# A residual decoder block on one core: the modulation rows of the down projection on another queue, and one weight sum on VectorE

## The chip, the cores and the metric

One Trainium2 chip, one core of it. The core has TensorE (PE, with its weight loads listed as PEld), VectorE (DVE), ScalarE (ACT), GpSimd (POOL) and SyncE (SP). SP, POOL and ACT can each issue transfers between memory and the core's buffers; the bytes are moved by the core's 16 data engines. The time is device time in microseconds; the kernel runs the whole block in one launch, float32 in and out.

## The reference

One decoder layer over 512 tokens of width 1024. The part that matters here is the end of the second sub-layer:

```python
h2 = rms_norm(x, norm2_g[l]) * (1 + scale2) + shift2
u = causal_dwconv(h2 @ w_up[l], conv_w[l], conv_b[l])
u_g, u_v = jnp.split(u, 2, axis=-1)
x = x + gate2 * ((jax.nn.silu(u_g) * u_v) @ w_down[l])
```

`gate2` is the sixth of six rows of width 1024 that come from `mod = c_act @ ada_w[l] + ada_b[l]`. `w_down` has 2816 rows and 1024 columns. Everything before (the first norm, the combined projection, attention, pooling, the merged output projection) and the up projection are not touched by the change.

## The kernel before, in words

The product with `w_down`, which is called the down projection here, is computed by a scheme with seven products of half-size blocks in place of eight. The weight matrix is cut into blocks b11, b12, b22, b21, the activation into a11, a12, a21, a22, and sums of blocks are formed on both sides. The seven products run one after the other as seven phases; `phases` lists them with the PSUM accumulators (X, Y or Z, two banks each) that they add into: a11·b11, s1·t1, s2·t2, a12·b21, s3·t3, s4·b22, a22·t4. The sums of weight blocks are t1 = b11 + b12, t2 = t1 + b22, t4 = t2 + b21 and t3 = b12 + b22. (The signs are taken care of on the activation side.)

A phase walks over six units (`NU`) of the contraction. Units 0 to 4 are 1024 columns wide in the buffer (two halves of 512), unit 5 is 512. Each number is kept as a high and a low part, so a weight unit is first split: ScalarE copies it to the high part `hi`, VectorE subtracts to get the low part `lo`, and TensorE does three matmuls where one would do. With two halves and two output tiles, a unit is 12 matmuls of 128x512. Buffers for `hi` and for `lo` are four each, so the split of a unit waits until TensorE is done with the unit four before it.

The work on TensorE, VectorE and ScalarE runs in the order in which the program is written. What the weights need is written ahead of their use: `d_ahead` splits two units ahead of TensorE, and `d_load` stands two units ahead of the split. The order of SP's and POOL's queues is set by a scheduler that follows the waits and the same order. Each queue issues in order, and an entry that waits holds up those behind it.

How the weight sums are made before the change: b11 is loaded into eleven buffers `ta` of 128x512, which stay for the whole down projection. When b11 has been split, POOL issues, for each `ta`, a transfer that adds b12 to it while it lands (`accum_op=ALU.add`, line 1367); when t1 has been split, one that adds b22; when t2 has been split, one that adds b21. So there are 33 such accumulating transfers of 256 KB. t3 is made in a buffer `raw_t`: SP loads b12 into it, then POOL adds b22 by an accumulating transfer of 512 KB (line 1349). b21 and b22 are plain loads by SP into `raw_b`. `raw_t`, `raw_b` and the columns of `ada_w` for the modulation all come from one pool of five buffers (`load_unit`, line 82); a load waits until the buffer's last reader is done.

The row gate2 is made like this: `ada_col(5, k)` loads an eighth of its weights and VectorE sums it into a column of `acol` (line 202); the last three of the eight stand in the second phase. At the end of the second phase `row_of(5, "g2")` has POOL write the eight columns to a row `g_d` in memory (line 837) and then load that row, repeated over all partitions, into two buffers `g` (line 842). VectorE multiplies with them in `finish`, for the first time at the start of the fifth phase.

Of the kernel before, what the change touches and what calls it, by code (L numbers as in the profile page):

```python
# [15 lines left out]
P = 128  # L16
# [39 lines left out]
def block_kernel(tc, x, cvec, ada, wtok, wch, pool_w, wbr, wout, wup, wdn, pack, table, out):  # L56
# [4 lines left out]
    with ctx:  # L61
# [771 lines left out]

        def row_of(g, name):

            gd = dpool.tile([1, D], F32, name=f"{name}_d")
            nc.gpsimd.dma_start(gd.rearrange("o (k p) -> p (o k)", p=P), acol[:, 8 * g : 8 * g + 8])
            rows = []
            for f in range(2):
                r = slot(f"{name}_{f}")  # L840
                src = gd[:, f * 512 : f * 512 + 512]
                nc.gpsimd.dma_start(r, bass.AP(tensor=src.tensor, offset=src.offset, ap=[[0, P], [1, 512]]))
                rows.append(r)
            return rows
# [33 lines left out]
        for j in range(8):  # L878
# [19 lines left out]
            if j == 6:  # L898
                g1 = row_of(2, "g1")

# [432 lines left out]
        ta, draw, dready, done = {}, {}, {}, [0, 0]  # L1333
        NEXT = {"b11": "b12", "t1": "b22", "t2": "b21"}

        def d_load(m):
# [4 lines left out]
            if nm == "b11":  # L1341
                ta[i] = [slot(f"ta_{i}_{u}") for u in range(w // 512)]
                for u, t in enumerate(ta[i]):
                    nc.sync.dma_start(t, src("b11", u * 512, u * 512 + 512))
            elif nm[0] == "b":
                draw[m] = load_unit(src(nm), f"{nm}_{i}")
            elif nm == "t3":
                draw[m] = load_unit(src("b12"), f"t3_{i}")
                nc.gpsimd.dma_start(draw[m], src("b22"), accum_op=ALU.add)

        def d_split(m):
# [7 lines left out]
            else:  # L1359
                parts = [(t, slice(u * 512, u * 512 + 512)) for u, t in enumerate(ta[i])]  # L1360
            for t, cs in parts:
                nc.scalar.activation(hi[:, cs], t, AF.Copy)  # L1362
            for t, cs in parts:
# [119 lines left out]
        for n, (an, bn, acc) in enumerate(phases):  # L1483
            last = n == len(phases) - 1
            held_ = []
            for i in range(NU):
# [18 lines left out]
                elif n == 1:  # L1505
                    if i in (1, 3, 5):
                        ada_col(5, 5 + i // 2)
# [8 lines left out]
                elif n == 3:  # L1516
                    split_a("s4", i)
                    split_a("a22", i)
            if last:
                for p, c0, c1 in ((1, 0, 256), (0, 0, 256), (1, 256, 512), (0, 256, 512)):  # L1520
# [6 lines left out]
            elif n == 1:  # L1527
                keep("s5", "Y")
                g2 = row_of(5, "g2")
            elif n == 2:  # L1530
# [80 lines left out]
```

## Time and profile before

| what | value |
|---|---|
| median of 3 runs | 674.3 us (673.5 to 674.65) |
| the profiled execution's own time | 671.35 us |
| its span | 669.5 us |
| PE, share of the span | 97% |
| DVE | 85% |
| ACT | 58% |
| POOL | 19% |

In the page, a group row reads: line, engine, operation, output<-inputs, count, then busy time and mean of one in ns, then the idle time of the engine just before and what ended it. In the timeline a row begins with the start in microseconds and the duration. In the windows view each engine's busy time in a stretch is given, and behind it the granted TensorE clock (1.00 is full), the busy share of the data engines and the rate in GB/s. In a queue row stand packets, MB, and the share of the 16 engines' time; a share can be a little over 100% since packets overlap. A matmul's listed duration is longer than the step from one start to the next, since matmuls are pipelined.

### The profile page before, as it was taken

The page shows a single profiled execution, that of the slowest core. Times are in us where ns is not written, and L with a number is a line of the kernel's source. Part 1 is how long each engine was busy: PE and PEld are TensorE (multiplying, and loading weights), DVE is VectorE, ACT ScalarE, POOL GpSimd, SP SyncE. Part 2 cuts the span into 40 slices and gives each one's busy share as a digit, 9 for nine tenths or more (in the row PEclk, how much of TensorE's full clock was granted, in tenths as well). Part 3 has the DMA queues.
Part 4 walks back from the last instruction along what each step waited for, and adds up shares of the span by engine and source line. Part 5 has one row for each costly group of instructions (what it writes and reads, how often), then busy time and mean ns, then how long its engine had stood idle before and what let it go on. Part 6 is the DMA issues. An engine that isn't in the chain of part 4 may idle for free.

```text
span 669.5 us, 9758 instructions
## 1 busy us (share of the span) xinstructions
PE 650.9 (97%) x3469; PEld 559.9 (84%) x3469; DVE 568.2 (85%) x990; ACT 390.2 (58%) x701; POOL 130.5 (19%) x164
## 2 busy tenths in 40 slices
PE   8999999999999999999999999999999999993997
PEld 6788788888888888888988989889898888882886
DVE  7997887988878868999799799998998989981785
ACT  8564436766655556566675657566565648571441
POOL 3004063432100146423000000000000017532100
PEclk9999999999999999999999999999999999996899
DMA  8986259999732876476522133332332679999921
GB/s 348 324 314 242 73 195 285 284 306 310 206 135 96 260 180 219 159 266 237 172 82 94 67 123 106 104 107 80 109 127 95 220 196 192 253 201 242 309 86 63
DMA packets 40583, 124.98 MB, mean 187 GB/s; under 512 B 5091, under 2 KB 5772, under 8 KB 40534
## 3 DMA queue, kind: packets, MB, share of 16 engines
q1 hardware_dynamic: 27638, 92.73, 40.1%
q0 software_dynamic: 12896, 31.63, 20.6%
q8 instruction: 27, 0.44, 0.3%
q14 instruction: 22, 0.18, 0.1%
HBM read 115.92 MB, written 8.42 MB: 186 GB/s over the span
## 4 chain that ended last, share of the span: by engine, by line
PE 88%; DMA 6%; DVE 2%; ACT 2%; issue 1%; POOL 1%; SPq 0%; DVEq 0%; POOLq 0%; ACTq 0%
PE u L129 6%; PE u L128 6%; PE u L130 6%; PE gate_ps L128 4%; PE gate_ps L130 4%; PE gate_ps L129 4%; PE uX L134 3%; PE uX L136 3%; PE uX L135 3%; PE X L135 2%; DMA g_d<-acol 2%; PE X L136 2%; PE X L134 2%; DMA raw_t<-in_wdn 2%; PE q L144 2%; PE p L144 2%
## 5 line engine op out<-in xcount | busy, mean ns | idle before, releaser
L128 PE MATMUL u<-h2h,hi_up 128*128 128x512 f32 (+1 forms) x216 | 78.3, 362 | 0.0
L129 PE MATMUL u<-h2l,hi_up 128*128 128x512 f32 (+1 forms) x216 | 78.2, 362 | 0.0
L130 PE MATMUL u<-h2h,lo_up 128*128 128x512 f32 (+1 forms) x216 | 78.1, 361 | 0.0
L1367 POOL DMA_DIRECT2D ta<-in_wdn x33 | 28.7, 1180 | 242.3 <-DVE lo_b L1364 222.7
L202 DVE CUSTOM_DVE_ANT_0 raw_ada<-raw_ada,cbc,pk 128x1024 f32<-128x1024 f32 x48 | 60.7, 1277 | 0.1
L128 PE MATMUL gate_ps<-h_h,hi_gate 128*128 128x512 f32 x128 | 50.1, 391 | 0.0
L130 PE MATMUL gate_ps<-h_h,lo_gate 128*128 128x512 f32 x128 | 50.0, 390 | 0.0
L129 PE MATMUL gate_ps<-h_l,hi_gate 128*128 128x512 f32 x128 | 50.0, 390 | 0.0
L130 PEld LDWEIGHTS u<-h2h,lo_up 128*128 128x128 f32 x216 | 40.8, 189 | 6.3
L128 PEld LDWEIGHTS u<-h2h,hi_up 128*128 128x128 f32 x216 | 40.8, 189 | 6.1
L129 PEld LDWEIGHTS u<-h2l,hi_up 128*128 128x128 f32 x216 | 40.8, 189 | 6.0
L130 PEld LDWEIGHTS gate_ps<-h_h,lo_gate 128*128 128x128 f32 x128 | 24.0, 188 | 5.1
L134 PE MATMUL X<-hi_t,s_h 128*128 128x512 f32 x44 | 18.2, 415 | 10.3 <-ACT hi_t L1362 10.3
L128 PEld LDWEIGHTS gate_ps<-h_h,hi_gate 128*128 128x128 f32 x128 | 24.0, 188 | 4.8 <-DVE mn L600 0.3
L129 PEld LDWEIGHTS gate_ps<-h_l,hi_gate 128*128 128x128 f32 x128 | 24.0, 188 | 4.6
L604 ACT ACTIVATE L<-L,mn 128x512 f32<-128x512 f32 (+3 forms) x32 | 17.6, 552 | 17.4 <-DVE mn L600 17.4
L109 ACT ACTIVATE hi_up<-raw_up 128x1024 fp32r<-128x1024 f32 x24 | 25.0, 1049 | 4.3 <-PE u L129 4.3
L1362 ACT ACTIVATE hi_t<-ta 128x512 fp32r<-128x512 f32 x33 | 19.3, 624 | 13.9 <-PE Y L136 7.5
L119 DVE TENSOR_TENSOR lo_gate<-raw_gate,hi_gate 128x1024 fp32r<-128x1024 f32 x16 | 19.5, 1221 | 6.6 <-ACT hi_gate L109 6.6
L1364 DVE TENSOR_TENSOR lo_t<-ta,hi_t 128x512 fp32r<-128x512 f32 x33 | 21.4, 686 | 3.9 <-ACT hi_t L1362 3.9
L1231 DVE TENSOR_TENSOR lo_up<-raw_up,hi_up 128x1024 fp32r<-128x1024 f32 x18 | 21.8, 1220 | 2.6 <-PE uY L136 2.0
L1364 DVE TENSOR_TENSOR lo_t<-raw_t,hi_t 128x1024 fp32r<-128x1024 f32 (+1 forms) x6 | 6.8, 1135 | 18.9 <-ACT hi_t L1362 18.7
(422 smaller groups left out, 2159.4 us busy)
## 6 DMA issues: line engine op xcount, KB each, us to landing
raw_ada<-in_ada SPq DMA_DIRECT2D x48, 512.0 KB, 4.9
raw_up<-in_wup SPq DMA_DIRECT2D x44, 512.0 KB, 3.2
ta<-in_wdn POOLq DMA_DIRECT2D x33, 256.0 KB, 9.7
raw_gate<-in_wch SPq DMA_DIRECT2D x16, 512.0 KB, 4.6
raw_b<-in_wdn SPq DMA_DIRECT2D x10, 512.0 KB, 5.7
ta<-in_wout POOLq DMA_DIRECT2D x16, 256.0 KB, 6.2
raw_br<-in_wbr SPq DMA_DIRECT2D x8, 512.0 KB, 4.2
raw_wo_t<-osum_t SPq DMA_DIRECT2D x8, 512.0 KB, 3.9
```

What stands on the lines that cost most here:

```text
L109: nc.scalar.activation(hi, raw, AF.Copy)
L128: nc.tensor.matmul(ps, sh, mh, start=start, stop=False)
L129: nc.tensor.matmul(ps, sh, ml, start=False, stop=False)
L130: nc.tensor.matmul(ps, sl, mh, start=False, stop=stop)
L134: nc.tensor.matmul(ps, sh, mh, start=start, stop=False, skip_group_check=True)
L135: nc.tensor.matmul(ps, sh, ml, start=False, stop=False, skip_group_check=True)
L136: nc.tensor.matmul(ps, sl, mh, start=False, stop=stop, skip_group_check=True)
L144: nc.tensor.matmul(ps, sl if i else sh, mh if i else ml, start=False, stop=stop and i != late)
L202: nc.vector.tensor_tensor_reduce(out=raw, in0=raw, in1=cbc, op0=ALU.mult, op1=ALU.add, scale=1.0, scalar=col(C_AB + i), accum_out=acol[:, ...
L1231: nc.vector.tensor_sub(lo, raw, hi.bitcast(F32))
L1364: nc.vector.tensor_sub(lo[:, cs], t, hi[:, cs].bitcast(F32))
L1367: nc.gpsimd.dma_start(t, wdn[plain[NEXT[nm]], i][:, cs], accum_op=ALU.add)
```

## The change

Three edits, all in the down projection.

1. `row_of` is cut in two. `row_out` (the write of `acol` to `g_d`, on POOL's queue) stays at the end of the second phase. `row_in` (the two loads of `g`) moves to the fourth phase, after the third unit's activation splits, and is issued from ScalarE's queue.
2. The last three `ada_col` calls in the second phase stand at units 0, 2, 4 in place of 1, 3, 5.
3. t4 is no longer made by accumulating transfers. The eleven transfers that added b21 into `ta` are gone (`"t2": "b21"` leaves `NEXT`). For the seventh phase b21 is loaded a second time, by SP into a `raw` buffer of the five-buffer pool, and VectorE adds `ta` (which holds t2) to it, one instruction for each half of 512, before ScalarE makes the high part.

```diff
-        def row_of(g, name):
+        def row_out(g, name):
 
             gd = dpool.tile([1, D], F32, name=f"{name}_d")
             nc.gpsimd.dma_start(gd.rearrange("o (k p) -> p (o k)", p=P), acol[:, 8 * g : 8 * g + 8])
+            return gd
+
+        def row_in(gd, name, eng):
             rows = []
             for f in range(2):
                 r = slot(f"{name}_{f}")
                 src = gd[:, f * 512 : f * 512 + 512]
-                nc.gpsimd.dma_start(r, bass.AP(tensor=src.tensor, offset=src.offset, ap=[[0, P], [1, 512]]))
+                eng.dma_start(r, bass.AP(tensor=src.tensor, offset=src.offset, ap=[[0, P], [1, 512]]))
                 rows.append(r)
             return rows
...
-        NEXT = {"b11": "b12", "t1": "b22", "t2": "b21"}
+        NEXT = {"b11": "b12", "t1": "b22"}
...
-            elif nm[0] == "b":
-                draw[m] = load_unit(src(nm), f"{nm}_{i}")
+            elif nm[0] == "b" or nm == "t4":
+                draw[m] = load_unit(src("b21" if nm == "t4" else nm), f"{nm}_{i}")
...
-            for t, cs in parts:
-                nc.scalar.activation(hi[:, cs], t, AF.Copy)
+            if nm == "t4":
+                raw = parts[0][0]
+                parts = [(raw[:, u * 512 : u * 512 + 512], slice(u * 512, u * 512 + 512)) for u in range(w // 512)]
+                for (r, cs), t in zip(parts, ta[i]):
+                    nc.vector.tensor_add(r, r, t)
+                    nc.scalar.activation(hi[:, cs], r, AF.Copy)
+            else:
+                for t, cs in parts:
+                    nc.scalar.activation(hi[:, cs], t, AF.Copy)
...
-                    if i in (1, 3, 5):
+                    if i in (0, 2, 4):
                         ada_col(5, 5 + i // 2)
...
+                    if i == 2:
+                        g2 = row_in(g2d, "g2", nc.scalar)
...
-                g2 = row_of(5, "g2")
+                g2d = row_out(5, "g2")
```

The order on POOL's queue before, from the middle of the t2 splits to the first sums for t3 (`ta` are the lasting buffers, `g_d` the row in memory, `g_0` and `g_1` the repeated row, `raw_t_0` the buffer of t3's first unit):

```order
L1367 DMA ta_1_5853<-in_wdn 128x512
L837 DMA g_d<-acol 128x8x1
L1367 DMA ta_0_5856<-in_wdn 128x512
L1367 DMA ta_1_5857<-in_wdn 128x512
L842 DMA g_0_6288<-g_d 128x512
L842 DMA g_1_6290<-g_d 128x512
L1367 DMA ta_0_5900<-in_wdn 128x512
L1367 DMA ta_1_5901<-in_wdn 128x512
L1367 DMA ta_0_5978<-in_wdn 128x512
L1367 DMA ta_1_5979<-in_wdn 128x512
L1367 DMA ta_0_5990<-in_wdn 128x512
L1349 DMA raw_t_0_6493<-in_wdn 128x1024
```

The same queue with the change, from the last sum for t2:

```order
L1377 DMA ta_1_5979<-in_wdn 128x512
L1377 DMA ta_0_5990<-in_wdn 128x512
L837 DMA g_d<-acol 128x8x1
L1352 DMA raw_t_0_6478<-in_wdn 128x1024
L1352 DMA raw_t_1_6509<-in_wdn 128x1024
L1352 DMA raw_t_2_6536<-in_wdn 128x1024
```

The first sum for t3 now follows the write of `g_d` directly; the two loads of `g` and the eleven sums for t4 are no longer on this queue.

On ScalarE, in the fourth phase, the two loads of `g` now stand between the third unit's activation split and the last b21 unit, ahead of t3's first unit:

```order
L1372 ACTIVATE hi_b_4_6481<-raw_b_4_6426 128x1024
L214 ACTIVATE s_2_h<-s_2_5029 128x512
L214 ACTIVATE a_2_h<-a_2_4708 128x512
L845 DMA g_0_6505<-g_d 128x512
L845 DMA g_1_6507<-g_d 128x512
L1372 ACTIVATE hi_b_5_6512<-raw_b_5_6452 128x512
L214 ACTIVATE s_3_h<-s_3_5639 128x512
L214 ACTIVATE a_3_h<-a_3_5162 128x512
L1372 ACTIVATE hi_t_0_6539<-raw_t_0_6478 128x1024
```

Before, those two DMA rows were not on ScalarE; the rest stood in the same order.

On VectorE, at the end of the sixth phase and in the seventh, with the change (`dt` are the finished output pieces):

```order
L1374 TENSOR_TENSOR lo_b_5_6773<-raw_b_5_6729,hi_b_5_6772 128x512
L1368 TENSOR_TENSOR raw_t_0_6752<-raw_t_0_6752,ta_0_5848 128x512
L1368 TENSOR_TENSOR raw_t_0_6752<-raw_t_0_6752,ta_1_5849 128x512
L1374 TENSOR_TENSOR lo_t_0_6791<-raw_t_0_6752,hi_t_0_6790 128x512 x2
L1368 TENSOR_TENSOR raw_t_1_6770<-raw_t_1_6770,ta_0_5852 128x512
L1368 TENSOR_TENSOR raw_t_1_6770<-raw_t_1_6770,ta_1_5853 128x512
L1374 TENSOR_TENSOR lo_t_1_6813<-raw_t_1_6770,hi_t_1_6812 128x512 x2
L1368 TENSOR_TENSOR raw_t_2_6788<-raw_t_2_6788,ta_0_5856 128x512
L1368 TENSOR_TENSOR raw_t_2_6788<-raw_t_2_6788,ta_1_5857 128x512
L1374 TENSOR_TENSOR lo_t_2_6833<-raw_t_2_6788,hi_t_2_6832 128x512 x2
L1463 TENSOR_TENSOR dt_1_0_6840<-Y_5974,s_0_6418 128x512
```

Before, the rows L1368 were not there, and the `lo_t` rows read `ta` directly.

More of the change, by code (lines that the diff above doesn't have):

```diff
@@ L898, in block_kernel @@
             if j == 6:
-                g1 = row_of(2, "g1")
+                g1 = row_in(row_out(2, "g1"), "g1", nc.gpsimd)
         nc.vector.scalar_tensor_tensor(acol[:, 32:40], acol[:, 32:40], 1.0, pk[:, C_N2 : C_N2 + 8],
```

## The prediction

> **What bounds the kernel now.** I first read the windows view over the down projection, which starts at 546.5 us of the span (columns: stretch, length, busy time of PE, PEld, DVE, ACT, POOL, granted clock, share of the data engines, GB/s):
>
> ```profile
> 600.00:610.00 10.00, 6.50 (x29) 5.07 (x27) 2.08 (x4) 0.74 (x2) 5.48 (x7) 0.96 1.07 316
> 610.00:620.00 10.00, 2.77 (x6) 1.87 (x7) 3.13 (x4) 3.77 (x6) 0.84 (x1) 0.50 1.09 211
> 620.00:630.00 10.00, 10.00 (x40) 8.09 (x39) 8.68 (x12) 3.18 (x3) 1.99 (x3) 0.86 1.04 308
> 630.00:640.00 10.00, 10.00 (x46) 8.29 (x45) 6.79 (x8) 5.49 (x6) 0.33 (x1) 1.00 0.69 233
> ```
>
> TensorE bounds the kernel everywhere but in one hole: from 606 to 617 it does nothing, then runs at half clock, while the data engines are full. The waits of TensorE over the last 170 us are only these two, and its timeline gives the edges of the hole:
>
> ```profile
> PE X L134 <- ACT hi_t L1362: 10.3, 1, 10.3
> PE X L135 <- DVE lo_t L1364: 0.5, 1, 0.5
> ```
>
> ```profile
> 605.89 0.39 PE L135 MATMUL Z<-lo_b,a_h 128*128 128x512 f32 x1
> 606.12 0.39 PE L136 MATMUL Z<-hi_b,a_l 128*128 128x512 f32 x1
> 616.77 0.79 PE L134 MATMUL X<-hi_t,s_h 128*128 128x512 f32 x1 [10.27 <-ACT hi_t L1362]
> ...
> 622.46 0.58 PE L136 MATMUL X<-hi_t,s_l 128*128 128x512 f32 x1
> 622.88 0.39 PE L134 MATMUL X<-hi_t,s_h 128*128 128x512 f32 x1
> ```
>
> A matmul starts every 0.227 us at full clock (605.89 to 606.12 rounds it), so the fifth phase was due at 606.35. Its first unit is 12 matmuls, 2.72 us, and the thirteenth matmul was due at 609.07. It started at 622.88. The hole therefore costs **13.8 us**: 10.4 of waiting, 3.4 of slow start. That is all that a better feed of the fifth phase can bring.
>
> Who made it wait stands in the chain that ended last (start, length, what):
>
> ```profile
> 580.04 15.94 DMA g_d<-acol
> ...
> 596.52 0.51 POOL g L842
> ...
> 600.82 14.74 DMA raw_t<-in_wdn
> 615.66 1.06 ACT hi_t L1362
> 616.75 1.24 DVE lo_t L1364
> 618.03 0.80 PE X L135
> ```
>
> and on POOL's queue:
>
> ```profile
> 569.95 2.66 POOL L1367 DMA_DIRECT2D ta<-in_wdn  x3 [1.61 <-DVE lo_t L1364]
> ...
> 596.51 1.11 POOL L842 DMA_DIRECT2D g<-g_d  x2 [10.96 <-DMA g_d<-acol]
> 597.62 4.44 POOL L1367 DMA_DIRECT2D ta<-in_wdn  x5
> 600.82 2.12 POOL L1349 DMA_DIRECT2D raw_t<-in_wdn  x1
> ```
>
> The sum for t3's first unit was issued at 600.82, because POOL stood 10.96 us for the write of the gate row and then issued the two row loads and five sums for t4. It took 14.74 us to land, because those transfers lay before it in the data engines.
>
> **The change part by part.** *The t4 sums and the row loads leave POOL's queue.* The next gate of t3's first sum is its own buffer's load by SP:
>
> ```profile
> 591.62 26.71 SPq L82 DMA_DIRECT2D raw_t<-in_wdn  x6
> 620.55 2.79 SPq L82 DMA_DIRECT2D raw_b<-in_wdn  x2
> ```
>
> It is issued at 591.62, when the buffer five loads earlier has been split, and the change does not move that. The landing of a 512 KB load, and of a 256 KB sum that had no sums queued ahead:
>
> ```profile
> raw_up<-in_wup SPq DMA_DIRECT2D x44, 512.0 KB, 3.2
> raw_t<-in_wdn SPq DMA_DIRECT2D x5, 512.0 KB, 7.5
> raw_t<-in_wdn POOLq DMA_DIRECT2D x1, 256.0 KB, 5.2
> ta<-in_wdn POOLq DMA_DIRECT2D x33, 256.0 KB, 9.7
> ```
>
> The load takes 3.2 (quiet) to 7.5 (crowded). I take about 3.6, landing at 595.2, since the last sum for t2 is issued by 572.6 (569.95 + 2.66) and even 15.94 us after that is 588.6, so the engines are free by 591. The sum that follows takes between 5.2 and the 14.74 of the chain. The price of the data comes from stretches in which one kind had the engines alone, 597 to 600 (plain loads) and 612 to 620 (sums of 512 KB):
>
> ```profile
> q1 hardware_dynamic: 330, 1.05, 100.0%
> q0 software_dynamic: 477, 1.70, 107.6%
> ```
>
> 512 KB are 0.524 MB, so a load costs 0.524 x 3.0/1.05 = 1.5 us of all data engines, and a sum 0.524 x 8.0/1.70 = 2.47. A first sum of 512 KB beside a load is then 5.2 + 1.24 + 1.5 = 7.9 us, landing at 603.1. ScalarE and VectorE need 1.06 + 1.24 (chain above), so the unit is ready at 605.4, before 606.35. The 10.4 us wait is gone, and with it the slow start, if no later wait is long: the clock fell 2.9 us after TensorE's last matmul.
>
> ```profile
> 608.00:609.00 1.00, 0.00 (x0) 0.00 (x0) 0.00 (x0) 0.00 (x0) 0.28 (x1) 1.00 1.11 221
> 609.00:610.00 1.00, 0.00 (x0) 0.00 (x0) 0.00 (x0) 0.00 (x0) 0.00 (x0) 0.60 1.15 209
> ```
>
> *What is late next: the other units of t3.* A unit costs the data engines 1.5 + 2.47 = 4.0 us, TensorE 2.72. Work until the fifth unit's sum is done: five loads 7.5, five sums 12.35, two gate row loads of 256 KB 1.5, the half load of the sixth unit 0.75, and one or two loads of b22, which start as t3's buffers come free (620.55 above, right behind the first split), 2.25. That is 24.35 us. They start near 592.5 and idle about 1.6 until the first sum's data begins, so they end at 618.4 and the sum lands near 619.3. Without waiting TensorE wants that unit at 606.35 + 4 x 2.72 = 617.23, that is, landed 2.3 earlier, at 614.9. So **4.4 us of waiting come back**, spread over four units in pieces of one to two us, each below the 2.9 after which the clock fell. The bounds are 0 (loads of b22 and rows fall into gaps) and the 8.5 of the second rival.
>
> Between ScalarE's queue and POOL's, the engines in use share about evenly, as 600.5 to 603 shows:
>
> ```profile
> q1 hardware_dynamic: 150, 0.55, 54.1%
> q0 software_dynamic: 146, 0.48, 49.7%
> ```
>
> Against the move of the rows speaks the Trainium skill, "DMA: Bandwidth & Descriptors", "Queues, rings and completion order" and "Issuing engines are not separate DMA queues": a data engine takes packets in turn from each queue row that has work, and ScalarE's is a row of its own on the same engines. By it the sums would get a third, not a half, while the 1.5 us of row loads are in flight, and lose (1/2 - 1/3) x 4.5 = 0.75 us more, 665.7 in place of 664.9. The trace of before has no third row, so it cannot show this.
>
> *The gate rows on ScalarE.* Two issues of at most 0.55 each (POOL's 1.11 for two) stand before the last b21 split, which ScalarE started at 599.07 after 0.93 of idle time:
>
> ```profile
> 599.07 0.63 ACT L1362 ACTIVATE hi_b<-raw_b 128x512 fp32r<-128x512 f32 x1 [0.93 <-DVE lo_b L1364]
> ```
>
> That idle time hides most of them; b21's last unit is due at 604.99 (606.35 less half a unit), and without the cover they would cost 1.1 of that slack, so nothing. They wait for the write of `g_d`. It is issued earlier now, since the last column sum is a unit sooner and fewer transfers lie ahead; even 15.94 us after 576 is 592, before ScalarE gets there.
>
> *The column sums one unit earlier.* Their number stays; each stands before one weight split that it followed:
>
> ```profile
> L202 DVE CUSTOM_DVE_ANT_0 raw_ada<-raw_ada,cbc,pk 128x1024 f32<-128x1024 f32 x48 | 60.7, 1277 | 0.1
> ```
>
> That split comes up to 1.28 us later. It is written two units, 5.4 us, ahead of its use, and TensorE's only waits are those above, so I take nothing; without that lead it would be 1.28 once, since VectorE's total is the same.
>
> *VectorE's eleven additions.* Nearest row, a subtraction of the same shape, and the idle time around it:
>
> ```profile
> 646.89 1.30 DVE L1364 TENSOR_TENSOR lo_t<-ta,hi_t 128x512 fp32r<-128x512 f32 x2 [1.39 <-ACT hi_t L1362]
> 649.61 1.29 DVE L1364 TENSOR_TENSOR lo_t<-ta,hi_t 128x512 fp32r<-128x512 f32 x2 [1.42 <-ACT hi_t L1362]
> ...
> 656.14 1.89 DVE L1364 TENSOR_TENSOR lo_t<-ta,hi_t 128x512 fp32r<-128x512 f32 x3
> 662.26 0.42 DVE L1455 TENSOR_TENSOR dt<-X,g 128x256 f32<-128x256 f32 x1 [4.24 <-PE X L136]
> ```
>
> ```profile
> 660.99 0.28 PE L134 MATMUL X<-hi_t,a_h 128*128 128x256 f32 x1
> ```
>
> Two in a row take 1.29, so one is 0.60 to 0.65, eleven 6.6 to 7.1. VectorE idles 1.39 + 1.42 in front of two splits (a wait for ScalarE that an addition can fill), and from 658.03 to 660.99, when TensorE takes up the last two units: 5.8. The rest, 0.8 to 1.3, falls on the last half unit, whose low part is wanted after the first six half-width matmuls, so about nothing shows. If each unit's subtraction also waited one conversion of 0.63 (the row at 599.07) for ScalarE, it would be 6 x 0.63 = 3.8 more, some 5 in all. The six extra loads by SP have five buffers' lead, 12 us, against a landing of 3.2 to 7.5. I take 0.
>
> **The sum.** 13.8 back, 4.4 lost again: 9.4 us. The profiled execution (671.35 with a span of 669.5) would come to 661.95, and the median of the runs, 2.95 above it, to **664.9**.
>
> **The rivals.**
> *All of it comes back* (0.18). For it: the fifth phase's own surplus is only a few us and the loads may find gaps. Against it: 4.0 us of data per unit against 2.72. Time 674.3 - 13.8 = 660.5.
> *One long wait remains, and the clock falls again* (0.14). With the crowded 7.5 for the load (599.1) and 10 for the sum, between 7.9 and 14.74, the first unit lands at 609.1 and is ready at 611.4: 5.1 us in one piece, and 3.4 for the slow start as measured above. 674.3 - 13.8 + 8.5 = 669.0.
> *VectorE becomes the bound of the last phase* (0.09). The six conversions of 0.63 that nothing fills come on top of the forecast: 664.9 + 3.8 = 668.7. For it: only about 6 us of idle time stand against 6.6 of additions. Against it: additions of the next unit stand right behind the subtractions and fill the wait.
> *ScalarE is held by the gate rows* (0.05). The new wait on an engine that converts: behind it stand the last b21 split and all of t3. It costs nothing until `g_d` lands after some 603, then each us costs one, and past 603 + 9.4 the kernel is slower. If POOL's write waits again behind transfers and lands 13 us past that point, at 616, the time is 664.9 + 13 = 678. Against it: 15.94 was with four t4 sums ahead, now gone.
> *The change does not reach the hole* (0.02), since something else held t3: about 674.
>
> **How the numbers follow.** The forecast itself has 0.52, with a range of its own from 662.5 to 667. From the full recovery with a little noise to the two cases at 669 the range is 660.3 to 669.5. Differences below 0.2% cannot be told from none here. Faster by more: 0.92; same: 0.03; slower: 0.05.
>
> **What would show it.** In the profile after: POOL's first `raw_t` sum issued near 595 to 597, no 10 us wait of X on `hi_t`, granted clock 1.00 throughout, several waits of one to two us on t3's units, and VectorE nearly without idle time in the last two phases while TensorE waits little there. One wait above 3 us with a clock of 0.50 behind it, or waits of TensorE on `lo_t` after 640, would make the forecast wrong.

## The result, and the profile after

| | before | with the change |
|---|---|---|
| median | 673.9 us (672.43 to 674.65, 4 runs) | 665.84 us (664.79 to 666.82, 4 runs) |
| profiled execution | 671.35 us, span 669.5 | 666.82 us, span 665.0 |
| ratio to before | 1 | 0.9883, 95% interval 0.9859 to 0.9906 |

The change is 1.2% faster, 0.9 us above the predicted 664.9 and inside the range. The two profiled executions are only 4.5 us apart, while the medians are 8.1 apart: the profile of before is at the low end of its runs, that of the change is the slowest of its four. The accounts below are of profiled executions; what that did to the forecast is told with its other steps.

The waits of TensorE from 500 us to the end, with the change (line it waits on, us in total, times, longest):

```profile
PE X L135 <- DVE lo_t L1374: 3.3, 7, 0.8
PE X L134 <- ACT hi_t L1369: 0.8, 1, 0.8
PE X L134 <- ACT hi_t L1372: 0.3, 1, 0.3
```

The one wait of 10.3 us and the one of 0.5 behind it have become nine short ones, the longest 0.84: six in the fifth phase and three in the last stretch of the seventh. The windows view of the same stretch (columns as in the prediction):

```profile
600.00:610.00 10.00, 8.97 (x39) 6.88 (x38) 4.70 (x7) 2.39 (x4) 2.52 (x3) 1.00 1.04 270
610.00:620.00 10.00, 8.75 (x36) 6.24 (x35) 7.64 (x11) 3.50 (x5) 2.25 (x3) 1.00 1.05 277
620.00:630.00 10.00, 9.11 (x40) 6.97 (x39) 7.06 (x8) 5.92 (x7) 0.56 (x1) 1.00 0.96 327
630.00:640.00 10.00, 10.00 (x46) 8.28 (x45) 9.49 (x14) 3.14 (x6) 1.07 (x2) 1.00 0.93 296
640.00:650.00 10.00, 10.00 (x46) 8.29 (x45) 9.37 (x15) 2.85 (x6) 0.00 (x0) 1.00 0.28 105
650.00:660.00 10.00, 8.59 (x42) 7.26 (x41) 6.40 (x13) 1.78 (x3) 0.00 (x0) 0.83 0.11 39
```

Where before stood 2.77 us of matmuls at a clock of 0.50 (610 to 620) there are now 8.75 at 1.00. The data engines are full all through the fifth phase (600 to 626.8), as they were. New are the last three rows: VectorE is nearly without a gap from 630 to 650, and then TensorE waits and its clock falls, in the last stretch of the kernel.

How much each stage lost can be read from the start of its first matmul. A full phase is 66 matmuls of 0.227 us, 14.96 us; the first four units of the seventh phase, 48 matmuls, take 10.88, and the last two units, which are done as 36 half-width matmuls and are called the tail here, take 4.19 from the first start to the last, which are also the values of before. With the change the fourth phase's last matmul starts at 606.30, so the fifth is due at 606.53; the sixth starts at 626.76, the seventh at 641.72, the tail at 652.60, and the last matmul at 660.72. So the fifth phase lost 626.76 - 606.53 - 14.96 = **5.3 us** (13.8 before), the sixth nothing, and the tail 8.12 - 4.19 = **3.9** (0 before). The sum is 9.2 us against 13.8, which is, within 0.1, the 4.5 us between the two spans.

The part of the chain of waits that answers to the one in the prediction (start, length, what):

```profile
592.48 3.76 DMA raw_t<-in_wdn
596.79 8.96 DMA raw_t<-in_wdn
605.85 1.07 ACT hi_t L1372
606.94 1.24 DVE lo_t L1374
```

and POOL's queue:

```profile
596.79 0.86 POOL L1352 DMA_DIRECT2D raw_t<-in_wdn  x1 [19.58 <-DMA raw_t<-in_wdn]
600.77 0.83 POOL L1352 DMA_DIRECT2D raw_t<-in_wdn  x1 [3.12 <-DMA g<-g_d]
```

The first sum for t3 is issued at 596.79 in place of 600.82, right behind its load, and lands in 8.96 us in place of 14.74. (The second row gives the landing of `g` as what the second sum waited for; the load of its buffer, issued at 594.60, landed 5.6 us later, within half a microsecond of it.) The first unit's low part is ready at 608.18 (606.94 + 1.24), 1.4 us after TensorE's second matmul wanted it (606.76); the rest of the 5.3 builds up in the sums that follow.

The tail, in TensorE's timeline (columns: start, length of the listed matmul, what; behind it the idle time before and what ended it):

```profile
652.60 0.28 PE L134 MATMUL X<-hi_t,a_h 128*128 128x256 f32 x1
653.11 0.38 PE L135 MATMUL X<-lo_t,a_h 128*128 128x256 f32 x1 [0.23 <-DVE lo_t L1374]
...
655.05 0.38 PE L134 MATMUL X<-hi_t,a_h 128*128 128x256 f32 x1 [0.84 <-ACT hi_t L1369]
655.78 0.39 PE L135 MATMUL X<-lo_t,a_h 128*128 128x256 f32 x1 [0.34 <-DVE lo_t L1374]
```

and VectorE's there:

```profile
650.84 1.28 DVE L1368 TENSOR_TENSOR raw_t<-raw_t,ta 128x512 f32<-128x512 f32 x2
652.36 1.29 DVE L1374 TENSOR_TENSOR lo_t<-raw_t,hi_t 128x512 fp32r<-128x512 f32 x2 [0.24 <-ACT hi_t L1369]
653.57 0.69 DVE L1368 TENSOR_TENSOR raw_t<-raw_t,ta 128x512 f32<-128x512 f32 x1
655.03 0.69 DVE L1374 TENSOR_TENSOR lo_t<-raw_t,hi_t 128x512 fp32r<-128x512 f32 x1 [0.78 <-ACT hi_t L1369]
```

TensorE comes to the last two units at 652.60, but VectorE adds the last of them only at 653.57, ScalarE has to convert the sum, and the last split ends at 655.72. The waits of TensorE sum to 1.4 us, and behind them it runs at half clock (columns as above):

```profile
654.00:655.00 1.00, 0.21 (x2) 0.00 (x1) 0.26 (x1) 0.63 (x1) 0.00 (x0) 1.00 0.00 0
655.00:656.00 1.00, 0.60 (x2) 0.41 (x3) 0.69 (x1) 0.00 (x1) 0.00 (x0) 1.00 0.00 0
656.00:657.00 1.00, 1.00 (x6) 1.00 (x6) 0.55 (x2) 0.00 (x0) 0.00 (x0) 0.53 0.00 0
657.00:658.00 1.00, 1.00 (x7) 1.00 (x6) 0.30 (x1) 0.00 (x0) 0.00 (x0) 0.50 0.00 0
658.00:659.00 1.00, 1.00 (x7) 1.00 (x7) 0.63 (x2) 0.00 (x0) 0.00 (x0) 0.50 0.39 131
659.00:660.00 1.00, 1.00 (x8) 1.00 (x8) 0.25 (x2) 0.00 (x0) 0.00 (x0) 0.77 0.00 0
```

The granted clock is below 1 from 656 to 660, which is another 1.7 us ((1 - 0.53) + (1 - 0.50) twice + (1 - 0.77)). So 2.2 of the 3.9 are waits and 1.7 are the clock. The clock did not fall like this in every execution of the change: the mean granted clock is 0.997 in the profiled one and 1.000, 0.999 and 1.000 in the other three, and 1.7 us at 665 would already be 0.0026. In those three the clock took less than that.

### The profile page after: what moved, and what is told of

Same layout as the page of the kernel before. It is cut to its first block, busy times and chain, and to the rows that moved or that the text cites. A ratio compares the mean times of both kernels' runs of the same rounds, so it can differ in the third digit from the quotient of the medians.

```text
span 665.0 us, 9760 instructions
## 1 busy us (share of the span) xinstructions
PE 653.4 (98%) x3469; PEld 560.1 (84%) x3469; DVE 574.8 (86%) x1001; ACT 390.3 (59%) x701; POOL 119.8 (18%) x151
## 4 chain that ended last, share of the span: by engine, by line
PE 84%; DMA 6%; DVE 6%; ACT 2%; issue 1%; SPq 0%; POOL 0%; ACTq 0%; DVEq 0%; POOLq 0%
PE u L129 6%; PE u L128 6%; PE u L130 6%; PE gate_ps L128 4%; PE gate_ps L129 4%; PE gate_ps L130 4%; DMA raw_t<-in_wdn 4%; PE uX L134 3%; PE uX L136 3%; PE uX L135 3%; PE q L144 2%; PE p L144 2%; PE X L135 2%; PE X L134 2%; PE X L136 2%; PE O L641 2%
## 5 line engine op out<-in xcount | busy, mean ns | idle before, releaser
L1377 POOL DMA_DIRECT2D ta<-in_wdn x22 | 19.1, 1159 | 238.4 <-DVE lo_b L1374 233.1
L1374 DVE TENSOR_TENSOR lo_t<-raw_t,hi_t 128x512 fp32r<-128x512 f32 (+1 forms) x17 | 14.0, 846 | 12.1 <-ACT hi_t L1372 10.2
L1246 ACT ACTIVATE hi_upR<-raw_up 128x512 fp32r<-128x512 f32 x20 | 12.6, 631 | 16.9 <-DVE raw_up L1271 9.5
L1151 ACT ACTIVATE ug<-ug 128x512 f32<-128x512 f32 x22 | 13.8, 629 | 13.1 <-DVE ug L1128 12.8
L135 PE MATMUL X<-lo_t,s_h 128*128 128x512 f32 x44 | 17.7, 402 | 2.8 <-DVE lo_t L1374 2.8
```

The source lines that it names most:

```text
L135: nc.tensor.matmul(ps, sh, ml, start=False, stop=False, skip_group_check=True)
L1377: nc.gpsimd.dma_start(t, wdn[plain[NEXT[nm]], i][:, cs], accum_op=ALU.add)
```

## The experiments

Ten kernels were run beside further runs of the kernel before. Each row below the second is the change with the edit that is shown under its name (t3_plain has the edit of late_finish as well); the lost times (us) are from the profiled execution, worked out as above. "Rest" is the span less all that was lost.

| kernel | median us | ratio to before (95%) | span | fifth | sixth | seventh with tail | rest |
|---|---|---|---|---|---|---|---|
| before | 673.9 | 1 | 669.5 | 13.8 | 0 | 0 | 655.7 |
| the change | 665.84 | 0.9883 (0.9859 to 0.9906) | 665.0 | 5.3 | 0 | 3.9 | 655.8 |
| sum_only | 666.24 | 0.9902 (0.9887 to 0.9918) | 664.3 | 7.1 | 0 | 1.5 | 655.8 |
| rows_only | 673.68 | 1.0009 (1.0001 to 1.0018) | 671.9 | 14.9 | 0.2 | 0 | 656.9 |
| no_adds | 663.49 | 0.9859 (0.9846 to 0.9871) | 662.1 | 5.9 | 0 | 0 | 656.2 |
| late_finish | 664.75 | 0.9874 (0.9861 to 0.9887) | 661.7 | 4.6 | 0 | 1.3 | 655.8 |
| sums_as_before | 666.81 | 0.9893 (0.9880 to 0.9907) | 665.2 | 5.8 | 0 | 3.5 | 655.9 |
| rows_from_sp | 666.79 | 0.9913 (0.9898 to 0.9928) | 664.4 | 7.1 | 0 | 1.5 | 655.8 |
| t3_plain | 663.49 | 0.9856 (0.9844 to 0.9869) | 661.3 | 3.9 | 0 | 1.6 | 655.7 |
| adds_on_pool | 669.19 | 0.9943 (0.9931 to 0.9955) | 669.1 | 6.0 | 0 | 6.9 | 656.2 |
| no_t3_sum | 659.66 | 0.9799 (0.9784 to 0.9814) | 657.3 | 0 | 0 | 1.5 | 655.9 |
| t3_plain_late_sums | 659.88 | 0.9801 (0.9787 to 0.9815) | 657.6 | 0 | 2.1 | 0 | 655.5 |

The last column is nearly one number, 655.5 to 656.9: to within 1.4 us, whatever a kernel here gains or loses stands in the three columns before it. Each row is a single execution, and the spans of one kernel differ among themselves, from 664.2 to 667.2 with rows_from_sp. So a difference of one or two microseconds between two rows does not show by itself what an edit did.

### Which edit brings it: sum_only and rows_only

sum_only is the third edit alone: the row is again loaded from POOL's queue at the end of the second phase, and the column sums stand where they stood.

```diff
-                    if i in (0, 2, 4):
+                    if i in (1, 3, 5):
...
-                    if i == 2:
-                        g2 = row_in(g2d, "g2", nc.scalar)
...
-                g2d = row_out(5, "g2")
+                g2 = row_in(row_out(5, "g2"), "g2", nc.gpsimd)
```

> Only the third edit: t4 by VectorE from a plain load; the gate row is written and loaded by POOL at the end of the second phase and the column sums stand at units 1, 3, 5, as before. Theory A (the hole came from the eleven t4 sums lying ahead of t3's first sum, and the move of the rows adds nothing): the write of the row lands near 590, the row loads run while the data engines are idle, t3's first sum is issued near 596 as in the changed kernel, and the time is that of the changed kernel or up to 1.5 us less, 664.3 to 666. Theory B (the 11 us that POOL stood for the write of the row made the hole, so the move is what counts): POOL issues t3's first sum several us later, 6 to 10 us of the hole stay, 670 to 674.

Measured: 666.24 us, 0.24 above theory A's bound, far below theory B's, and with overlapping intervals no different from the whole change. POOL's queue:

```profile
577.61 0.96 POOL L837 DMA_DIRECT2D g_d<-acol  x1 [5.18 <-DVE acol L202]
589.34 1.10 POOL L845 DMA_DIRECT2D g<-g_d  x2 [10.77 <-issue]
596.53 0.88 POOL L1352 DMA_DIRECT2D raw_t<-in_wdn  x1 [6.09 <-DMA raw_t<-in_wdn]
```

POOL stands 10.77 us for the row, as it stood 10.96 before (this view names no cause; the write of `g_d` landed 11.2 us after its issue, at 588.8), and is free at 590.4, six microseconds before t3's load has landed. The row cost nothing by itself. What stood behind it before were t4's sums, and t3's behind those.

rows_only is the first two edits alone: t4 is made by accumulating transfers again.

```diff
-        NEXT = {"b11": "b12", "t1": "b22"}
+        NEXT = {"b11": "b12", "t1": "b22", "t2": "b21"}
...
-            elif nm[0] == "b" or nm == "t4":
+            elif nm[0] == "b":
...
-            if nm == "t4":
+            if False:
```

> Only the first two edits: rows loaded from ScalarE's queue in the fourth phase, column sums a unit earlier; t4 by accumulating transfers as before. Theory A: the eleven sums still fill the data engines until after 600, t3's first load is crowded (near 7 us) and its first sum lands near 608, so TensorE waits some 4 to 5 us in one piece, the clock falls, and later units wait too; nothing is lost on VectorE in the last phase: 667 to 671. Theory B: POOL no longer stands still, t3's first sum is issued near 596 and the hole closes as in the changed kernel, without its loss at the end: 661 to 664.

Measured: 673.68 us, above both theories: nothing gained. The wait of TensorE is back whole, and POOL's queue and the chain show why:

```profile
PE X L134 <- ACT hi_t L1372: 11.1, 1, 11.1
```

```profile
587.07 3.44 POOL L1377 DMA_DIRECT2D ta<-in_wdn  x4 [2.45 <-DVE lo_t L1374]
595.27 1.72 POOL L1377 DMA_DIRECT2D ta<-in_wdn  x2 [4.76 <-DMA g_d<-acol]
605.48 0.84 POOL L1352 DMA_DIRECT2D raw_t<-in_wdn  x1 [8.48 <-DMA raw_t<-in_wdn]
```

```profile
593.27 11.65 DMA raw_t<-in_wdn
605.48 12.23 DMA raw_t<-in_wdn
```

POOL is done with t4's sums at 597, 4 us sooner than before, but those sums now fill the data engines while SP's plain load for t3 is under way. The load takes 11.65 us (3.76 in the change), and t3's sum cannot be issued before it. So the two edits on the row are worth nothing, alone or with the third. It is the eleven t4 sums in the data engines ahead of t3 that made the hole, more than their place on POOL's queue.

### Where the column sums and the row stand: sums_as_before and rows_from_sp

```diff
-                    if i in (0, 2, 4):
+                    if i in (1, 3, 5):
```

> The change with the last three column sums back at units 1, 3 and 5 of the second phase, where they stood before. It tests what the early column sums do to t3's first load, which was issued at 592.48 with the change and at 591.62 before. Theory A (the chain runs through VectorE: an early column sum delays the t1 split, by that the sum for t2, by that the last b21 split, and by that the buffer of t3's first load): the load is issued near 591.6 again, the first t3 unit is ready 0.9 sooner, and the fifth phase loses 4.4 in place of 5.3: 665.0 against 665.8. Theory B (the fifth phase's loss is set by the data engines' 4.0 us per unit; an earlier start only lets the engines begin earlier, or the row of the gate comes later and falls among t3's loads): the time stays within 0.5 of 665.8, or rises by up to 1.5 since the write of the gate row is issued a unit later.

Measured: 666.81 us, and t3's first load is issued at 592.29 (592.48 in the change, 591.62 before). Theory A falls: the column sums are not what delayed the load by 0.9, and what did was not found. Theory B is left: within its bound, 1.0 above the change with overlapping intervals. Part of that 1.0 may be the clock: three of its five executions have a mean granted clock of 0.996 and spans of 665.0 to 665.2, the other two 0.999 and 1.000 and spans of 662.6 and 663.3.

```diff
-                        g2 = row_in(g2d, "g2", nc.scalar)
+                        g2 = row_in(g2d, "g2", nc.sync)
```

> The change with the two loads of the repeated gate row issued from SyncE's queue in place of ScalarE's, at the same place of the program. Theory A (which queue they are on does not matter: 1.5 us of data-engine work either way; the third row with its own share costs nothing that shows): within 0.5 of 665.8. Theory B (a third queue takes its own share of the engines from the sums): the third row is gone, the sums land up to 0.75 sooner, 665.1. Theory C (on SyncE's in-order queue they wait for the write of the gate row and hold up the loads of t3 behind them): t3's load comes later than 592.5 and the fifth phase loses more, 667 to 669.

Measured: 666.79 us. It is 0.95 above the change with overlapping intervals, so between A and C by its time; B, the gain, did not come. Its fifth phase lost 7.1, with one wait of 1.6 us on the third unit, and behind it the clock fell:

```profile
PE X L134 <- ACT hi_t L1372: 1.6, 1, 1.6
```

```profile
618.00:620.00 2.00, 2.00 (x7) 1.52 (x6) 0.68 (x1) 0.96 (x1) 0.57 (x1) 0.50 1.05 231
```

The clock is at 0.50 from 617.6 to 621.0, which is 1.7 of the 7.1; without it some 5.4 would be left, as with the change (5.3).

SP issued the row loads at 597.32, between t3's third load and its fourth. That moved the crowding and did not remove it: t3's second sum was issued at 598.87 in place of 600.77, its third at 605.66 in place of 604.49. A third queue that shares the data engines is not what the change loses by.

### What the additions cost: no_adds, late_finish, adds_on_pool

no_adds leaves the eleven additions out, so its seventh product uses b21 in place of t4.

```diff
-                    nc.vector.tensor_add(r, r, t)
```

> The changed kernel without VectorE's eleven additions, so the seventh product uses b21 in place of t4; everything else, the six extra loads too, stays. As predicted (additions cost nothing): same time as the changed kernel, within 0.7 us. By the changed kernel's profile (3.9 us lost in the last 4 to 8 us of TensorE's work, where it waits for the split of the last two units and then runs at half clock): 2 to 4 us less, 662 to 664, no wait of TensorE on the split after 640 and the last 36 half matmuls in 4.2 us.

Measured: 663.49 us, 2.35 below the change by medians (its spans are 661.1 to 662.2, those of the change 663.0 to 665.0). The tail loses nothing. That the medians give 2.35 and the profile of the change 3.9 fits the 1.7 us of clock, which the other executions of the change did not lose in full. VectorE's gaps are those of before, twice this one:

```profile
639.52 1.29 DVE L1373 TENSOR_TENSOR lo_t<-raw_t,hi_t 128x512 fp32r<-128x512 f32 x2 [1.43 <-ACT hi_t L1368]
```

late_finish moves the finishing of the sixth product, two times three VectorE instructions (4.1 us), behind the last split.

```diff
-                if due:
+                if due and (not last or i > 3):
                     due.pop(0)()
+                    if last and due:
+                        due.pop(0)()
```

> The changed kernel with the finishing of the sixth product (two times three VectorE instructions, 4.1 us) written behind the last split of the seventh phase in place of between its third, fourth and fifth. If what makes the last two units late is VectorE's order, the splits of units 3 to 5 come 2 to 4 us earlier and the loss at the end goes: 2 to 4 us less than the changed kernel, 662 to 664, close to the run without additions. If it is the additions' own chain through ScalarE (two additions, conversion, subtraction, unit by unit), the loss stays: 665 to 666.

Measured: 664.75 us, between the two expectations and 1.1 below the change by medians, with intervals that overlap. In the profile there is no wait for the seventh phase's splits any more; a new one stands in its place:

```profile
PE X L134 <- DVE dt L1465: 1.0, 1, 1.0
```

That is TensorE waiting to write the second half of an accumulator that VectorE, late with its finishing, is still reading. The same VectorE work is late at another place: 1.3 us stay lost in the tail.

adds_on_pool gives the eleven additions to GpSimd.

```diff
-                    nc.vector.tensor_add(r, r, t)
+                    nc.gpsimd.tensor_add(r, r, t)
```

> The change with the eleven additions of the seventh phase on GpSimd in place of VectorE. The nearest row for GpSimd is its subtraction of 128x512 in the same kernel, 1.52 us, against 0.65 on VectorE. Theory A (the 2.4 us that leaving out the additions brought are VectorE's time): GpSimd has 5.4 us per two units and needs 3.0 per unit, so the additions run a little ahead or a little behind; the loss of the tail, 3.9, falls to 0 to 1.5 and the time is 663 to 664.5. Theory B (GpSimd's additions are slower than TensorE's 2.72 per unit, 3.0 per unit, and slow VectorE down while they run): waits of TensorE on hi_t in the seventh phase, 0.3 more for each unit, and VectorE's 0.65 rises; 665.5 to 668.

Measured: 669.19 us, above both theories. TensorE waits 5.3 us in one piece, not on the additions but on one of VectorE's splits:

```profile
PE X L135 <- DVE lo_t L1374: 7.7, 5, 5.3
```

```profile
636.09 2.31 DVE L1374 TENSOR_TENSOR lo_b<-raw_b,hi_b 128x1024 fp32r<-128x1024 f32 x1
640.03 1.77 DVE L1374 TENSOR_TENSOR lo_t<-raw_t,hi_t 128x512 fp32r<-128x512 f32 x1
641.73 8.02 DVE L1374 TENSOR_TENSOR lo_t<-raw_t,hi_t 128x512 fp32r<-128x512 f32 x1
```

```profile
641.78 7.42 POOL L1368 TENSOR_TENSOR raw_t<-raw_t,ta 128x512 f32<-128x512 f32 x6
```

The subtraction that began at 641.73 took 8.02 us: it ended at 649.75, just behind GpSimd's run of six additions (641.78 to 649.20). The splits that ran beside GpSimd's first four additions took 1.77 us for 512 columns and 2.31 for 1024 (1.22 otherwise), and the four behind the long run 0.68 each, as without GpSimd. Theory B had a part of the mechanism, that GpSimd slows VectorE; it expected waits on hi_t, and its size was far too small. The clock then was at half from 649.3 to 652.7, which cost TensorE another 1.4 us or so. GpSimd's own additions took 1.45 us on average, 1.24 in the run of six, less than the 1.52 they were costed at. The Trainium skill, "GPSIMD Engine Reference", "1. Specifications", states that GpSimd's way to the buffer is shared with VectorE and contends with VectorE instructions that have two inputs there. The trace agrees: such an instruction took 1.77 to 8.02 us in place of 0.68.

### What is left in the fifth phase: t3_plain, no_t3_sum, t3_plain_late_sums

t3_plain is late_finish with t3 made as t2 - b11 by VectorE from a plain load.

```diff
-                draw[m] = load_unit(src("b12"), f"t3_{i}")
-                nc.gpsimd.dma_start(draw[m], src("b22"), accum_op=ALU.add)
+                draw[m] = load_unit(src("b11"), f"t3_{i}")
...
+                    if nm == "t3":
+                        nc.vector.tensor_sub(r, t, r)
```

> The kernel late_finish (finishing of the sixth product behind the last split of the seventh phase; 664.75), and t3 made as t2 - b11 by VectorE from a plain load of b11, so that the fifth phase has no accumulating transfers. Theory A (what remains lost in the fifth phase, 4.6 in late_finish, is the data engines' 1.5 + 2.47 us per unit against TensorE's 2.72): with 1.5 per unit the first unit is ready long before it is due and the data engines are half idle; the loss of the fifth phase falls to at most 2, and the time is 660.5 to 662.5. VectorE then does 1.29 more per unit in the fifth phase: 7.1 us of additional work, which its idle time there takes. Theory B (VectorE cannot take eleven more subtractions in the fifth phase, where it also finishes the fourth product): waits of TensorE on lo_t take the place of the waits on hi_t, several of 1 to 2 us, and the time is 664 to 667.

Measured: 663.49 us, between the two theories, and the profile shows a part of each. The data engines' share falls from 1.04 to 0.47 (600 to 610) and the first three units start without a wait. The fourth and fifth wait:

```profile
PE X L134 <- ACT hi_t L1371: 2.3, 2, 1.3
```

```profile
612.15 0.68 DVE L1462 TENSOR_TENSOR dt<-Z,s 128x512 f32<-128x512 f32 x1
...
614.20 1.29 DVE L1368 TENSOR_TENSOR raw_t<-ta,raw_t 128x512 f32<-128x512 f32 x2
```

VectorE finishes the fourth product first and comes to the fourth unit's subtraction only at 614.20. It has no idle time of more than 0.8 us from 602 to 651. The limit has moved from the data engines to VectorE.

no_t3_sum takes the disputed cost away without giving VectorE any work: the six sums of t3 are left out.

```diff
-                nc.gpsimd.dma_start(draw[m], src("b22"), accum_op=ALU.add)
```

> The change with the six accumulating transfers of t3 left out: t3 is then b12 alone, so the fifth product is not the one of the scheme, and what is left of the fifth phase is plain loads of 1.5 us of data-engine work per unit. So far the loss of the fifth phase and that of the tail add up to 8.5 to 9.3 in every kernel that has the eleven additions on VectorE in the tail (5.3 + 3.9 with the change, 7.1 + 1.5 with rows_from_sp and sum_only). Theory A (the data engines make the first loss, and the tail's loss follows from it: VectorE gets t3's last units 2 to 3 us late, starts the sixth phase's splits late and never catches up): both losses go, fifth phase 0 to 0.5, tail 0 to 1, time 660 to 661. Theory B (VectorE's work behind the fifth phase is too much by itself): fifth phase 0 to 0.5, tail 4 to 8, since TensorE comes to it earlier while VectorE does not: 664 to 666.

Measured: 659.66 us, just below theory A's 660. The fifth phase loses nothing, so its 5.3 us are the accumulating transfers of t3. The tail loses 1.45, above A's 0 to 1 and far below B's 4 to 8, although all eleven additions are there. Before the second and the third b22 split VectorE now waits, where in the change it ran through:

```profile
618.75 1.23 DVE L1373 TENSOR_TENSOR lo_b<-raw_b,hi_b 128x1024 fp32r<-128x1024 f32 x1 [1.50 <-ACT hi_b L1371]
621.47 1.23 DVE L1373 TENSOR_TENSOR lo_b<-raw_b,hi_b 128x1024 fp32r<-128x1024 f32 x1 [1.49 <-ACT hi_b L1371]
```

In the change VectorE has no gaps from b22's first split (625.41) to the end of t4's last (655.72) but the waits for the conversions, 1.9 us in all. That stretch is 30.3 us (30.4 to 30.7 in the next three kernels of the table), and TensorE wants the last split 26.65 us after the start of the sixth phase (10.88 + 14.96 to the tail, then seven half-width matmuls). So the split is late by some 3.7 us less VectorE's lead, that is, the time by which b22's first split starts ahead of the sixth phase:

| kernel | b22's first split | sixth phase starts | lead | t4's last split ends | late by | lost in the tail |
|---|---|---|---|---|---|---|
| the change | 625.41 | 626.76 | 1.35 | 655.72 | 2.3 | 3.9 |
| sums_as_before | 625.18 | 627.31 | 2.13 | 655.86 | 1.9 | 3.5 |
| sum_only | 626.04 | 628.43 | 2.39 | 656.40 | 1.3 | 1.5 |
| rows_from_sp | 626.21 | 628.59 | 2.38 | 656.56 | 1.3 | 1.5 |
| no_t3_sum | 616.03 | 621.54 | 5.51 | 649.51 | 1.3 | 1.5 |

The table accounts for the tail, one execution to a row. The lead goes with the landing of t3's last unit, and not with what the fifth phase loses in all: in the change the conversion of that unit waited 2.34 us for the transfer, and VectorE 1.75 for the conversion; in sum_only it had landed in time, and VectorE waited 0.73. A lateness of 1.3 costs 1.5; at 1.9 and 2.3 it costs about as much as it is, and TensorE's clock falls as well, which is another 1.7 us. With t3 in time the lead is 5.5, but VectorE then waits 3.0 us at b22's second and third split, and 1.3 of lateness stay: theory A is right on the fifth phase and on a part of the tail, and 1.5 us are VectorE's own. It is also why the two losses add up to nearly the same in the kernels that the expectation lists: where TensorE is held longer in the fifth phase, VectorE gains lead. The near equality is also chance, since the sums hold 1.7 us of clock in the tail of the change, 1.7 in the fifth phase of rows_from_sp, and none with sum_only.

t3_plain_late_sums joins the two: t3 by VectorE from a plain load, the finishing of the fourth product behind t3's last split, and t4 by accumulating transfers again. Those add into the buffers from which t3 is subtracted, so they now have to wait for t3.

```diff
-            elif nm[0] == "b" or nm == "t4":
+            elif nm[0] == "b":
...
-            if nm == "t4":
+            if nm == "t3":
...
-                    nc.vector.tensor_add(r, r, t)
+                    nc.vector.tensor_sub(r, t, r)
...
+            if nm == "b22":
+                for u, t in enumerate(ta[i]):
+                    nc.gpsimd.dma_start(t, wdn[plain["b21"], i][:, u * 512 : u * 512 + 512], accum_op=ALU.add)
...
-                if due:
+                if due and (n != 4 or i > 2):
```

> t3 made as t2 - b11 by VectorE from a plain load, as in t3_plain; t4 again by eleven accumulating transfers into the lasting buffers, which now have to wait until VectorE has read t2 for t3 in the fifth phase, so they cannot lie ahead of t3; the finishing of the fourth product stands behind t3's last split. VectorE's work is 7.1 us less than in t3_plain, in which it had no idle time from 594 to 651. Theory A (in t3_plain VectorE was the limit, and the data engines are free in the sixth phase): waits of TensorE on the first units of t3 and b22 only, 0.3 to 1.2 in all, none in the tail: 660 to 661.5. Theory B (eleven sums of 1.24 us and five and a half loads of 1.5 of b22 from 604 to 626 fill the data engines and the sums land late, as they did in before): waits on hi_b or hi_t in the sixth and seventh phases of 2 to 6 us, 662.5 to 667.

Measured: 659.88 us, 2.0% faster than before and 0.8% faster than the change by the two ratios (0.9801 / 0.9883). Its time is 0.1 below theory A's range and far from theory B's; the waits, 0.3 to 1.2 by theory A, came to 1.5, and 2.1 us were lost:

```profile
PE Y L135 <- DVE lo_b L1371: 1.5, 2, 1.3
```

```profile
619.66 0.68 DVE L1460 TENSOR_TENSOR dt<-Z,s 128x512 f32<-128x512 f32 x1
...
621.72 1.22 DVE L1371 TENSOR_TENSOR lo_b<-raw_b,hi_b 128x1024 fp32r<-128x1024 f32 x1
```

Its data engines are full from 610 to 630 (shares 1.01 and 1.09) and nobody waits for them there. The one wait is for VectorE, which finishes a piece of the fourth product at 619.66, ahead of b22's first split.

## Why the prediction was right, and where it was not

| step of the prediction | forecast | measured |
|---|---|---|
| the hole of the fifth phase comes back | 13.8 | 13.8 (no wait over 0.8, clock 1.00 there) |
| first unit of t3 | ready at 605.4, no wait | 608.2, waits of 0.3 and 0.8 |
| lost again over t3's units | 4.4 | 5.3 |
| gate rows on ScalarE's queue | 0 | 0, and nothing gained by them |
| column sums a unit earlier | 0 | within 1 us, no gain in undoing it |
| VectorE's eleven additions | 0 | 3.9 in the profile, of which 1.7 by the clock; 2.4 by the medians |
| from the profiled execution to the median | + 2.95 | - 0.98 |

**The main step was right.** The one long wait and the half clock behind it are gone, and what returns in the fifth phase is the data engines' work for t3: without the sums the phase loses nothing. The steps between the first five conversions of t3 (605.85, 609.71, 613.03, 616.07, 620.40) are 3.64 us on average against the 4.0 that were worked out per unit and TensorE's 2.72. The pieces came as 0.2 to 0.8 us of listed waiting and not as one to two us each, since each unit's first low part is waited for by itself.

**The first unit was mis-sized by 2.8 us.** The load was issued 0.9 later than the prediction said it must be, the sum was issued 0.55 us behind the landing, and it took 8.96 us and not 7.9. In the loss of the whole phase 0.9 shows (5.3 against 4.4); that the data engines' work sets the rest is argued from their full share.

**The step that failed is the term of VectorE's eleven additions, taken at 0.** Eleven additions of 0.65 were measured as 7.1 us together, as costed. Against them stood 2.8 us of gaps and the slack before the last split is wanted, 3.8. What the sum lacked were the waits for ScalarE's conversion, 0.23 us in five units and 0.78 in the last, 1.9 in all: they were put into a rival with a chance of 0.09, and "about nothing shows" was said of a remainder that had no reserve. The argument against that rival, that the next unit's additions fill the wait, does not hold for the order in which VectorE works: between a unit's additions and its subtractions nothing else stands. Reckoned from the start of the sixth phase, the last split ended at 22.9 us before (658.03 - 635.15) and ends at 29.0 now (655.72 - 626.76): 6.1 later, which is 7.1 + 1.9 - 2.8 within 0.1. It is wanted at 26.65, so the slack was 3.8 and the split is 2.3 late. In the profiled execution the clock's fall adds 1.7. The prediction named exactly this sign as the one that would make it wrong, waits on lo_t after 640, and they are there (0.23 and 0.34 us), with a wait of 0.84 on hi_t between them. Had the third rival been added to the forecast and not set against it, the sum would have been 668.7, too high by 2.9, for the next reason.

**The near hit of the total owes something to two errors that cancel.** The sum gave a span of 660.1 (669.5 - 9.4), and the four spans of the change are 663.0 to 665.0, some 4 us higher. The 2.95 us that were added to come from the profiled execution to the median made up for most of that. It was taken as something that the change leaves alone. In every run here the time is 1.7 to 1.9 us above the span, so the 2.95 lay inside the span; most later runs of before have spans of 670 to 672, and the one that was profiled, at 669.5, was a short one. By the constant rest of 655.7 a typical run of before, at 671.5, loses about 15.8, not 13.8. That the extra 2 us lie in the hole is an inference from the constant rest of the profiled runs; no run of before with a long span was profiled.

**The rivals.** Full recovery, 660.5, is what the change would have given without t3's sums (659.66). One long wait with a second fall of the clock did not come in the fifth phase. VectorE as the bound of the last phase came, with 3.9 us in place of 3.8, but by another sum: 2.2 of waits, behind which stand the 1.9 of conversions that nothing fills, and 1.7 of clock. ScalarE was not held: it issued the two row loads at 594.50, and its first t3 conversion, at 605.85, had waited 5.95 us for the transfer alone.

The sum by the rule of a third queue, 665.7, is near the 665.84 by accident: taking that queue away brought nothing. The even shares of 600.5 to 603, by which it was reckoned, are those of SyncE's queue and POOL's, and not ScalarE's, which moved nothing there.

## What to carry to other kernels

Work that is taken off a full resource should be costed on the engine that receives it up to its deadline: additions, the new waits for the engine between them, less the gaps, against the slack of the last instruction, and a remainder without reserve is not zero. Of three edits that all touch one wait, ask which of them frees the resource that is full; here it was the data engines, and moving entries of a queue past each other gained nothing while the same bytes still went first. When all losses of a kernel can be put into a few stages, check that the rest stays constant from kernel to kernel, and forecast the losses of a typical run and not only those of the profiled one.

## What the runs showed of the hardware that was not expected

GpSimd's additions held up VectorE's instructions with two buffers as inputs: 1.77 us in place of 0.68 beside some, and a single one of 8.02 us beside a run of six. So a piece of work of 7.1 us moved from VectorE to GpSimd cost 3.35 us more in the end (669.19 against 665.84).

TensorE's clock fell in the tail after waits of no more than 0.84 us each. It was idle or nearly so only from 654.2 to 655.8, and the clock fell at 656; at the hole of before it fell 2.9 us after the last matmul. With rows_from_sp it fell at 617.6, behind waits of 1.62 and 0.76. So the clock can fall although each single wait is well below 2.9 us, which the prediction took as safe. In t3_plain one wait of 1.4 us in the tail left it at 1.00:

```profile
654.84 0.39 PE L134 MATMUL X<-hi_t,a_h 128*128 128x256 f32 x1 [1.37 <-DVE dt L1467]
```

```profile
650.00:660.00 10.00, 5.89 (x42) 5.26 (x40) 7.53 (x15) 0.00 (x0) 0.00 (x0) 1.00 0.30 105
```

The Trainium skill, "TensorE: Matmul & The Clock Gate", "Part 1: The HAM clock gate", states that activity is judged over a window of about 3.4 us that runs freely, so the moment within it matters. The trace agrees in so far as the same 1.4 us of waiting had unlike effects; an idle stretch of 3.4 us was not there. Each of the four falls that were looked at here also lasted 3.4 us at half clock, and so cost up to 1.7 us (the change, sums_as_before, rows_from_sp, adds_on_pool), and the hole of before 13.6, four times that.

A plain load of 512 KB takes 3.76 us when the data engines are free of sums, and 11.65 us in rows_only, where six accumulating transfers of 256 KB were issued between 587 and 597. The two row loads ran beside it in both.
